# ConvFFN down: sixteen of its 22 blocks as seven products of 512 columns, with the sums of its weights made by DMA in DRAM

## The chip, the cores and the metric

One core of a Trainium2 chip runs the whole program. The metric is the device time of one execution in microseconds (us). Before the change the median of three runs is 840.73 us, from 840.38 to 840.88.

## The reference, cut to what matters

The reference is one decoder block on 512 tokens of 1024 channels: a conv branch and a gated recurrent branch are merged, projected and normalized (x1), and a ConvFFN follows. The change is in its last product and in the residual that is added to it:

```python
x = layer_norm(ALPHA * x + mix, ln1_g, ln1_b)
z = x @ w_ffn_in                        # 1024 -> 5632
u, gv = jnp.split(z, [D_FF], axis=-1)   # D_FF = 2816 = 22 blocks of 128
u = causal_dwconv(u, w_ffn_dw, b_ffn_dw)
y_ffn = (jax.nn.gelu(u) * gv) @ w_ffn_out   # 2816 -> 1024
x = layer_norm(ALPHA * x + y_ffn, ln2_g, ln2_b)
```

All of it is float32. The kernel multiplies in fp32r and splits each operand into a high part (a cast to fp32r) and a low part (the operand less its high part); a product is then three matmuls, high by high, high by low and low by high.

## The kernel before, in words

**Products.** `mm3` (L157) issues the three matmuls of a product (L159 to L161). `split` (L150) makes the two parts of an operand: ScalarE casts (L152), VectorE subtracts (L155).

**Weights.** All weights lie in one DRAM tensor of tiles of 128 x 1024 float32 (512 KB). `fetch(i)` (L113) loads tile i by SyncE's queue into a buffer `raw`, of which there are three (L119); ScalarE casts it to `hi` (L140) and VectorE subtracts to `lo` (L141). There are five buffers of `hi` and five of `lo`. For the tiles 8 to 67 the low part is made in another way (L127 to L129): ScalarE casts, ScalarE writes -hi into `lo`, and GpSimd issues a DMA that adds `raw` to `lo`; that tile's `raw` is free only when this DMA has landed. `weight(i)` (L144) fetches up to three tiles ahead.

**Order of the work.** The program is written in one order, and a planner puts the instructions of every engine and every DMA queue into a fixed order from that, by when its own model says that they are ready. Each queue then works strictly in order, and an instruction that waits holds up what is behind it.

**ConvFFN up** (L945 to L966). Blocks 0 to 2 are plain. For each of the blocks 3 to 21 the product is done with seven half-size products instead of eight (`seven`, L614; `seven_up`, L918). The sums of weights for that are made on VectorE (`weight_sums`, L583) from two tiles `d` and `e`, which SyncE's queue loads (L590): t13 is a difference of both (L594), t24 two more (L605, L606), and every one is split. `prepare(j + 1)` is written ahead of block j, so that a block's weights are made during the block before. Each block ends in `act` (L909), which writes the hidden block hT[j]. The last of the seven products of a block (`finish`, L656) is kept back in `pending` and issued inside the next block, since it adds to the bank X that VectorE has to read first (L654).

**ConvFFN down** (L969 to L1039). The 22 hidden blocks are split (`hidden`), and for the blocks k = 0 to 15 every weight tile is multiplied with four token blocks and two halves of 512 columns: 24 matmuls of 512 columns. Ahead of that stand two large loads: the 2 MB residual `x1a` from the DRAM copy `x1_d` (L978), and the four rows of gains and biases `lnp` (L970). The gain and bias of the first norm are put on the residual here (L1007, L1008). The `finish` of block 21 is issued after two of the four token blocks of k = 0 (L1017). The blocks 16 to 21 come last, token block by token block, each followed by its norm and its store.

Of the kernel before, what the change touches and what calls it, by code (L numbers as in the profile page):

```python
# [60 lines left out]
W_N = W_FO + 22  # L61


@with_exitstack
def hybrid_block(ctx: ExitStack, tc: tile.TileContext, wts: bass.AP, xT_d: bass.AP,
# [44 lines left out]

    resident = {}

    def fetch(i):  # L113
# [4 lines left out]
        for c in pieces:  # L118
            nc.sync.dma_start(raw[:, c], wts[i][:, c])  # L119
# [673 lines left out]

    x1_d = ctx.enter_context(tc.tile_pool(name="dram", bufs=1, space=bass.MemoryType.DRAM)).tile([T, D], F32, name="x1_d")
    x1 = [p1p.tile([P, 1024], F32, tag=f"oh{tb}", name=f"x1_{tb}") for tb in range(NT)]
# [26 lines left out]

    keep = {}

    def ln1_transposes(half, tb, n):
# [29 lines left out]
    for half in range(2):  # L855
# [11 lines left out]
        for tb in tbs:  # L867
# [3 lines left out]
            normalize(x1[tb], f"a{tb}")  # L871
            nc.sync.dma_start(x1_d[tb * P:tb * P + P, :], x1[tb])
# [5 lines left out]
    NK = 16  # L878
    hT = {}

    def hid():

        for tag, c0, n in [("ch", 0, 4), ("cl", 4, 4)] + [(f"sc{i}", 8 + 2 * i, 2) for i in range(4)]:
# [3 lines left out]
        for c in range(16, NFF):  # L887
            hT[c] = tmp.tile([P, T], F32, tag=("tot", "kt", "gg")[(c - 16) // 2], name=f"hT{c}")
# [40 lines left out]
    def prepare(j):  # L929
        i = W_FI + 2 * j  # L930
        if j in PLAINS:
# [5 lines left out]
            return [loaded.pop(i), loaded.pop(i + 1)]  # L937
        t = [p1p.tile([P, 1024], F32, tag=tag, name=f"T{tag}_{j}") for tag in ("oh2", "oh3")]
        b21 = [tmp.tile([P, T], F32R, tag=tag, name=f"b{tag}_{j}") for tag in ("kT", "t1")]
        return weight_sums(i, t, b21, ("oh0", "oh1"))  # L940

# [8 lines left out]
    for i in range(2):  # L950
        factor_sums(i, sh, sl)
    hid()
    for j in range(NF):
        act(j, *pss[2 * j:2 * j + 2])
    assert state[0] == W_FI + 2 * PLAIN, state
    for j in range(NF, NFF):
        if j == NF:
            w = prepare(j)
        wn = prepare(j + 1) if j + 1 < NFF else None
        if j in PLAINS:  # L960
# [7 lines left out]

    lnp = p1p.tile([P, 4, 1024], F32, tag="xl", name="lnp")  # L969
    po.dma_start(lnp, ln_d.unsqueeze(0).broadcast_to([P, 4, 1024]))  # L970
    bks = [4, 5, 0, 1, 2, 3, 6, 7]
    yps = {}

    res = p1p.tile([P, 4, 1024], F32R, tag="xh", name="fores")
    resident[W_FO + NK] = lambda: (res[:, 0], res[:, 1])
    resident[W_FO + NK + 1] = lambda: (res[:, 2], res[:, 3])
    x1a = p1p.tile([P, NT, 1024], F32, tag="ol", name="x1a")
    nc.sync.dma_start(x1a, x1_d.rearrange("(b p) c -> p b c", p=P))  # L978
    hres = [p1p.tile([P, 2, T], F32R, tag=f"sv{i}", name=f"hres{i}") for i in range(4)]
    hsp = {}  # L980

    def hidden(k):

        if k not in hsp:
            if NK <= k < NK + 4:
                hi, lo = hres[k - NK][:, 0], hres[k - NK][:, 1]
            else:
                if k % 2:
                    hl = tmp.tile([P, 2, T], F32R, tag="qq", name=f"hq{k}")
                    hi, lo = hl[:, 0], hl[:, 1]  # L990
                else:
                    hi, lo = [tmp.tile([P, T], F32R, tag=t, name=f"h{t}{k}") for t in ("kT", "t1")]
            split(hi, lo, hT[k])
            hsp[k] = (hi, lo)
        return hsp[k]

    def down(k, w, tb, ns=(0, 1)):
        hi, lo = hidden(k)
        ts = slice(tb * P, tb * P + P)
        for n in ns:  # L1000
            c = slice(n * 512, n * 512 + 512)
            mm3(yps[tb][n], (hi[:, ts], lo[:, ts]), (w[0][:, c], w[1][:, c]), k == 0, k == NFF - 1)

    for k in range(NK):
        if 2 <= k < 2 + NT:
            x_ = x1a[:, k - 2]
            ve.tensor_tensor(x_, x_, lnp[:, 0], ALU.mult)  # L1007
            ve.tensor_tensor(x_, x_, lnp[:, 1], ALU.add)  # L1008
        if k == 0:
            hidden(0)  # L1010
        w = weight(W_FO + k)
        for kk in range(k, min(k + 3, NK) if k else 1):
            hidden(kk)
        for tb in range(NT):
            if k == 0:
                if tb == 2:
                    pending.pop()()  # L1017
                yps[tb] = [bank(bks[2 * tb + n]) for n in range(2)]
            down(k, w, tb)
    ws = [weight(W_FO + k) for k in range(NK, NFF)]  # L1020
    for k in range(NK, NFF):
        hidden(k)
    for tb in range(NT):
        for n in range(2):
            for k in range(NK, NFF):
                down(k, ws[k - NK], tb, (n,))
        st = sml.tile([P, 2, 6], F32, tag="lst", name=f"lstb{tb}")
# [3 lines left out]
        for n, c in enumerate(halves):  # L1031
            ve.scalar_tensor_tensor(x1a[:, tb, c], x1a[:, tb, c], ALPHA, yps[tb][n], ALU.mult, ALU.add)
            ve.bn_stats(st[:, n], x1a[:, tb, c])
        ve.bn_aggr(mv, st.rearrange("p a b -> p (a b)"))
        rsqrt(rs, mv[:, 1:2], 1, 1.0, LN_EPS, f"b{tb}")
        for c in halves:
            ve.scalar_tensor_tensor(x1a[:, tb, c], x1a[:, tb, c], mv[:, 0:1], lnp[:, 2, c], ALU.subtract, ALU.mult)
            ve.scalar_tensor_tensor(x1a[:, tb, c], x1a[:, tb, c], rs, lnp[:, 3, c], ALU.mult, ALU.add)
            nc.sync.dma_start(out[tb * P:tb * P + P, c], x1a[:, tb, c])  # L1039


def pack(inp):
# [68 lines left out]
```

## Time and profile before

| | |
|---|---|
| median of three runs | 840.73 us |
| the profiled execution | 840.79 us, of which the span is 839.0 us |
| TensorE busy | 821.0 us of the span |
| VectorE, ScalarE, GpSimd busy | 617.0, 460.6 and 87.8 us |
| ConvFFN up, seven products | from about 517 us to 708.6 us, one block each 10.08 us |
| ConvFFN down | from 708.6 us to 830 us, then the norm of the last token block |

The span is the time from the first to the last instruction in the profile; the 1.8 us around it are in the run's time alone. PE stands for TensorE's matmuls, DVE for VectorE, ACT for ScalarE, POOL for GpSimd and SP for SyncE, whose name with a q is its DMA queue. Busy times overlap a little: a matmul is counted from its start until its result is out, though the next one starts before that, and so is a VectorE instruction. A rate is therefore read from starts that follow each other. In brackets a row gives how long the engine was idle before, and what ended it.

### The profile page before, as it was taken

The page shows a single profiled execution, that of the slowest core. Times are in us where ns is not written, and L with a number is a line of the kernel's source. Part 1 is how long each engine was busy: PE and PEld are TensorE (multiplying, and loading weights), DVE is VectorE, ACT ScalarE, POOL GpSimd, SP SyncE. Part 2 cuts the span into 40 slices and gives each one's busy share as a digit, 9 for nine tenths or more (in the row PEclk, how much of TensorE's full clock was granted, in tenths as well). Part 3 has the DMA queues.
Part 4 walks back from the last instruction along what each step waited for, and adds up shares of the span by engine and source line. Part 5 has one row for each costly group of instructions (what it writes and reads, how often), then busy time and mean ns, then how long its engine had stood idle before and what let it go on. Part 6 is the DMA issues. An engine that isn't in the chain of part 4 may idle for free.

```text
span 839.0 us, 14550 instructions
## 1 busy us (share of the span) xinstructions
PE 821.0 (98%) x5771; PEld 719.7 (86%) x5771; DVE 617.0 (74%) x1113; ACT 460.6 (55%) x820; POOL 87.8 (10%) x147
## 2 busy tenths in 40 slices
PE   8999999999999999999999999999999999999995
PEld 6888778777777778999978899999999999888884
DVE  5369999955587638788474689689998999844356
ACT  4455555667678865566641556566666666423200
POOL 0112431433332400000100000000000000000000
PEclk9999999999999999999999999999999999999998
DMA  8688666654543664233675332323333234634101
GB/s 287 177 180 206 167 148 155 166 135 128 130 126 98 170 171 138 76 104 110 162 242 187 115 113 76 95 84 104 118 106 101 101 102 161 271 121 130 46 26 75
DMA packets 32995, 113.40 MB, mean 135 GB/s; under 512 B 3616, under 2 KB 4512, under 8 KB 32800
## 3 DMA queue, kind: packets, MB, share of 16 engines
q1 hardware_dynamic: 24288, 82.85, 29.6%
q0 software_dynamic: 6480, 25.17, 14.9%
q10 hardware_dynamic: 2160, 4.47, 1.5%
q8 instruction: 45, 0.74, 0.4%
q14 instruction: 22, 0.18, 0.1%
HBM read 85.21 MB, written 4.19 MB: 107 GB/s over the span
## 4 chain that ended last, share of the span: by engine, by line
PE 78%; DVE 12%; ACT 4%; DMA 3%; issue 1%; DVEq 0%; ACTq 0%; POOLq 0%; SPq 0%
PE ps L159 25%; PE ps L160 24%; PE ps L161 24%; DVE cws L262 6%; DMA wr<-in_wts 2%; DMA xr<-in_xT 1%; PE ps L379 1%; ACT wh L127 1%; PE ps L528 1%; DVE tt L412 1%; PE ps L530 1%; PE ps L543 1%; DMA wl<-wr 1%; PE ps L517 1%; PE ps L492 0%
## 5 line engine op out<-in xcount | busy, mean ns | idle before, releaser
L159 PE MATMUL ps<-xh,wh 128*128 128x512 f32 x256 | 104.4, 409 | 0.5 <-ACT xh L152 0.4
L160 PE MATMUL ps<-xl,wh 128*128 128x512 f32 x256 | 100.9, 394 | 0.5 <-DVE xl L155 0.5
L161 PE MATMUL ps<-xh,wl 128*128 128x512 f32 x256 | 100.4, 392 | 0.0
L262 DVE SCALAR_TENSOR_TENSOR cws<-cws,par 128x512 f32<-128x512 f32 x120 | 84.8, 756 | 0.1
L140 ACT CAST wh<-wr 128x1024 fp32r<-128x1024 f32 x34 | 35.6, 1049 | 61.3 <-PE ps L161 34.3
L141 DVE TENSOR_TENSOR wl<-wr,wh 128x1024 fp32r<-128x1024 f32 (+1 forms) x38 | 43.2, 1139 | 34.7 <-ACT wh L140 34.4
L127 ACT CAST wh<-wr 128x1024 fp32r<-128x1024 f32 x44 | 46.4, 1057 | 39.1 <-PE ps L160 27.8
L159 PE MATMUL ps<-sh,shi_t 128*128 128x256 f32 x228 | 64.5, 283 | 0.0
L160 PE MATMUL ps<-sl,shi_t 128*128 128x256 f32 x228 | 64.5, 283 | 0.0
L161 PE MATMUL ps<-sh,slo_t 128*128 128x256 f32 x228 | 64.5, 283 | 0.0
L129 POOL DMA_DIRECT2D wl<-wr x44 | 38.6, 877 | 225.4 <-ACT wl L128 205.3
L159 PEld LDWEIGHTS ps<-xh,wh 128*128 128x128 f32 x256 | 48.2, 188 | 12.0 <-ACT xh L152 1.9
L161 PEld LDWEIGHTS ps<-xh,wl 128*128 128x128 f32 x256 | 48.1, 188 | 10.2
L160 PEld LDWEIGHTS ps<-xl,wh 128*128 128x128 f32 x256 | 48.2, 188 | 9.8 <-DVE xl L155 1.2
L155 DVE TENSOR_TENSOR slo_t<-Toh,shi_t 128x1024 fp32r<-128x1024 f32 x38 | 46.4, 1221 | 12.6 <-ACT shi_t L152 11.9
L152 ACT CAST shi_t<-Toh 128x1024 fp32r<-128x1024 f32 x38 | 39.9, 1050 | 16.7 <-PE ps L160 8.3
L128 ACT ACTIVATE wl<-wh 128x1024 fp32r<-128x1024 f32 x44 | 46.6, 1059 | 0.8
L159 PEld LDWEIGHTS ps<-sh,shi_t 128*128 128x128 f32 x228 | 43.8, 192 | 0.0
L160 PEld LDWEIGHTS ps<-sl,shi_t 128*128 128x128 f32 x228 | 43.8, 192 | 0.0
L161 PEld LDWEIGHTS ps<-sh,slo_t 128*128 128x128 f32 x228 | 43.8, 192 | 0.0
L568 ACT COPY pc<-ps 128x256 f32<-128x256 f32 x57 | 21.2, 372 | 37.0 <-PE ps L161 36.8
L155 DVE TENSOR_TENSOR slo_b<-wr,shi_b 128x1024 fp32r<-128x1024 f32 x27 | 32.9, 1218 | 2.4 <-ACT shi_b L152 2.4
(384 smaller groups left out, 2552.4 us busy)
## 6 DMA issues: line engine op xcount, KB each, us to landing
wr<-in_wts SPq DMA_DIRECT2D x141, 512.0 KB, 3.8
wl<-wr POOLq DMA_DIRECT2D x44, 512.0 KB, 4.9
xr<-in_xT ACTq DMA_DIRECT2D x8, 256.0 KB, 5.2
x<-in_x ACTq DMA_DIRECT2D x4, 512.0 KB, 9.9
x_d<-x SPq DMA_DIRECT2D x4, 512.0 KB, 4.1
x1a<-x_d SPq DMA_DIRECT2D x1, 2048.0 KB, 8.4
lnp<-in_ln POOLq DMA_DIRECT2D x1, 2048.0 KB, 10.6
out<-x1a SPq DMA_DIRECT2D x8, 256.0 KB, 2.0
```

What stands on the lines that cost most here:

```text
L127: ac.copy(hi, raw)
L128: ac.mul(lo, hi, -1.0)
L129: po.dma_start(lo, raw, accum_op=ALU.add)
L140: ac.copy(hi[:, c], raw[:, c])
L141: ve.tensor_tensor(lo[:, c], raw[:, c], hi[:, c], ALU.subtract)
L152: ac.copy(hi, src)
L155: (lo_eng or ve).tensor_tensor(lo, src, hi, ALU.subtract)
L159: pe.matmul(ps, a[0], b[0], start=start, stop=False, skip_group_check=more)
L160: pe.matmul(ps, a[0], b[1], start=False, stop=False, skip_group_check=more)
L161: pe.matmul(ps, a[1], b[0], start=False, stop=stop, skip_group_check=more)
L262: ve.scalar_tensor_tensor(cacc[j], cpad[j][:, i:i + T], w, cacc[j], ALU.mult, ALU.add)
L568: f(*args)
```

## The change: what it does, and its diff

- The blocks 0 to 15 of down are a product of 512 tokens by 2048 hidden channels by 1024 columns. It is cut in two in each of the three directions and done with seven products instead of eight. Each product has four weight tiles, and each tile gets 12 matmuls of 512 columns.
- Three of the seven weight operands are tiles of the input (b11, b21, b22). Four are sums of such tiles (t1 to t4): they are made in DRAM during up, by DMA copies on SyncE's queue and adding DMAs on GpSimd's. Four 64-byte DMAs ahead of the copies read hT[j-2], so that a copy can't go before that is written.
- So 34 tiles are fetched in down instead of 22. Of each four tiles the last (DMA_LOW) gets its low part by ScalarE, ScalarE and an adding DMA, like the tiles 8 to 67.
- The sums of hidden blocks (`operand`) are made on VectorE, and their parts by `split`. One of the two results of a token and column quarter is collected in the bank, the other is added to x1a on the way (`take_sum`).
- The gain and bias of the first norm go onto x1 before it is stored to x1_d (`residual`): for token blocks 0 and 1 among the steps that run beside up's start, for 2 and 3 (`late`) after `prepare(3)`. x1a now takes the buffer `xl`, which the `finish` of block 21 reads, and that `finish` is issued after three matmuls of down instead of twelve.

```diff
+FOP = ("b11", "b21", "t1", "t2", "b22", "t3", "t4")
+W_S = W_FO + 4 * len(FOP) + 6
+DMA_LOW = 3
...
+    def source(i):
+        if i < W_FO:
+            return wts[i]
+        n = i - W_FO
+        if n >= 4 * len(FOP):
+            return wts[W_FO + NK + n - 4 * len(FOP)]
+        t, m = FOP[n // 4], n % 4
+        return wts[W_FO + FO_OF[t] + m] if t in FO_OF else tsum[t][m]
...
-        if 8 <= i < W_OUT and i not in resident:
+        if (8 <= i < W_OUT or i >= W_FO and (i - W_FO) % 4 == DMA_LOW) and i not in resident:
...
+    def residual(tb):
+        ve.tensor_tensor(x1[tb], x1[tb], gb1[0], ALU.mult)
+        ve.tensor_tensor(x1[tb], x1[tb], gb1[1], ALU.add)
+        nc.sync.dma_start(x1_d[tb * P:tb * P + P, :], x1[tb])
...
+    def fo_sums(j):
+        fo = lambda t, m: wts[W_FO + FO_OF[t] + m]
+        m = j - NF - 1
+        if 0 <= m < 4:
+            for t, b in (("t1", "b12"), ("t3", "b12"), ("t2", "b22"), ("t4", "b21")):
+                nc.sync.dma_start(tsum[t][m][0:1, 0:16], hT[j - 2][0:1, 0:16])
+                nc.sync.dma_start(tsum[t][m], fo(b, m))
+        m, c = divmod(j - NF - 3, 3)
+        if 0 <= m < 4:
+            if c == 0:
+                po.dma_start(tsum["t1"][m], fo("b11", m), accum_op=ALU.add, max_dma_last_dim=4096)
+                po.dma_start(tsum["t3"][m], fo("b22", m), accum_op=ALU.add, max_dma_last_dim=4096)
+            elif c == 1:
+                po.dma_start(tsum["t2"][m], tsum["t1"][m], accum_op=ALU.add, max_dma_last_dim=4096)
+            else:
+                po.dma_start(tsum["t4"][m], tsum["t2"][m], accum_op=ALU.add, max_dma_last_dim=4096)
     for j in range(NF, NFF):
+        fo_sums(j)
         if j == NF:
             w = prepare(j)
+            for f in late:
+                f()
...
-    for k in range(NK):
...
-        for tb in range(NT):
...
-            down(k, w, tb)
+    ops = operand("b11")
+    for n, t in enumerate(FOP):
+        nxt = None
+        for m in range(4):
+            w = weight(W_FO + 4 * n + m)
+            if m == 1 and n + 1 < len(FOP):
+                nxt = operand(FOP[n + 1])
+            for c in range(2):
+                first, end = m == 0 and c == 0, m == 3 and c == 1
+                for i in range(2):
+                    if n == 0 and first:
+                        if i:
+                            pending.pop()()
...
+                    hi, lo = (o[:, c, i * P:i * P + P] for o in ops[m])
+                    cs = slice(c * 512, c * 512 + 512)
+                    mm3(C[i, into[t]], (hi, lo), (w[0][:, cs], w[1][:, cs]), new and first, end, not new)
+        for i in range(2):
+            take_sum(t, i)
+        ops = nxt
```

The banks of the four quarters are X, W and Z per token half: b11, t2, t3 and t4 go into X, b21 into W, t1 and b22 into Z; t2, b22, t3 and t4 add to what stands there. The six blocks behind the seven products and the norm are as before, but for the residual that has been added to three of the four quarters already, and for the rows of gain and bias, of which two (gb2) are loaded instead of four.

## Rows read from the trace of the kernel before

**Rows 1.** The page: the span, and the busy time of each engine.
```profile
span 839.0 us, 14550 instructions
PE 821.0 (98%) x5771; PEld 719.7 (86%) x5771; DVE 617.0 (74%) x1113; ACT 460.6 (55%) x820; POOL 87.8 (10%) x147
```
**Rows 2.** The chain of waits, 690 to 839 us: start us, us, what.
```profile
714.12 0.23 PE ps L161
...
737.24 0.23 PE ps L161
...
829.72 0.24 PE ps L161
829.99 0.70 DVE x1a L1032
...
835.08 0.66 DVEq L1107
```
**Rows 3.** Stretches of up and down: us, busy times (count), TensorE clock, DMA share, GB/s.
```profile
550.00:600.00 50.00, 50.00 (x419) 50.00 (x418) 45.21 (x59) 31.07 (x50) 0.00 (x0) 1.00 0.33 106
708.00:829.00 121.00, 121.00 (x544) 100.53 (x543) 69.43 (x104) 31.49 (x41) 0.56 (x1) 1.00 0.34 120
```
**Rows 4.** Groups by line and shape, 480 to 839 us: busy us, mean ns.
```profile
L141 DVE TENSOR_TENSOR wl<-wr,wh 128x1024 fp32r<-128x1024 f32 x20 | 24.4, 1222 | 21.8 <-ACT wh L140 21.7
L140 ACT CAST wh<-wr 128x1024 fp32r<-128x1024 f32 x20 | 20.9, 1048 | 28.8 <-PE ps L161 20.2 <-issue 4.1 <-DMA wr<-in_wts 3.8
```
**Rows 5.** The page's groups: ScalarE writes -hi into the low part.
```profile
L128 ACT ACTIVATE wl<-wh 128x1024 fp32r<-128x1024 f32 x44 | 46.6, 1059 | 0.8
```
**Rows 6.** VectorE in order of time, one block of up (555 to 582 us).
```profile
565.78 1.23 DVE L155 TENSOR_TENSOR slo_t<-Toh,shi_t 128x1024 fp32r<-128x1024 f32 x1 [0.80 <-ACT shi_t L152]
...
569.17 1.22 DVE L594 TENSOR_TENSOR Toh<-wr,wr 128x1024 f32<-128x1024 f32 x1
...
572.12 1.22 DVE L155 TENSOR_TENSOR slo_b<-wr,shi_b 128x1024 fp32r<-128x1024 f32 x1
573.25 0.68 DVE L606 TENSOR_TENSOR Toh<-wr,Toh 128x512 f32<-128x512 f32 x1
573.85 1.22 DVE L155 TENSOR_TENSOR slo_t<-Toh,shi_t 128x1024 fp32r<-128x1024 f32 x1
```
**Rows 7.** ScalarE in order of time, the same block.
```profile
567.09 0.62 ACT L152 CAST bkT<-wr 128x512 fp32r<-128x512 f32 x1 [0.21 <-DMA wr<-in_wts]
```
**Rows 8.** DMA queues, 150 to 300 us: packets, MB, share of 16 engines.
```profile
q0 software_dynamic: 2736, 9.96, 34.2%
q1 hardware_dynamic: 2880, 10.22, 20.3%
```
**Rows 9.** Line 119, 150 to 300 us: issue to landing of the weight loads.
```profile
DMA to landing us min/median/max: 3.3/3.4/5.8
```
**Rows 10.** Line 129, 150 to 300 us: GpSimd's issues (ns), and their landing.
```profile
L129 POOL DMA_DIRECT2D wl<-wr x20: 855/879/1122, 151.7 to 299.2; - x20
...
DMA to landing us min/median/max: 4.4/4.8/7.4
```
**Rows 11.** ScalarE, 437 to 450 us: casts of weight tiles that come each 2.7 us.
```profile
442.03 1.05 ACT L140 CAST wo_ol<-wr 128x1024 fp32r<-128x1024 f32 x1 [2.18 <-DMA wr<-in_wts]
444.70 1.05 ACT L140 CAST wh<-wr 128x1024 fp32r<-128x1024 f32 x1 [1.62 <-DMA wr<-in_wts]
448.13 1.05 ACT L140 CAST wh<-wr 128x1024 fp32r<-128x1024 f32 x1 [2.38 <-DMA wr<-in_wts]
```
**Rows 12.** The start of down as a stretch, columns as in group 3.
```profile
716.00:720.00 4.00, 4.00 (x19) 3.33 (x18) 3.31 (x5) 2.24 (x4) 0.00 (x0) 1.00 1.05 440
```
**Rows 13.** ScalarE at the start of down.
```profile
723.39 1.05 ACT L140 CAST wh<-wr 128x1024 fp32r<-128x1024 f32 x1 [3.76 <-DMA wr<-in_wts]
```
**Rows 14.** TensorE where up ends and down begins.
```profile
708.50 0.28 PE L161 MATMUL ps<-sh,slo_t 128*128 128x256 f32 x1
708.62 0.40 PE L159 MATMUL ps<-wh,hkT 128*128 128x512 f32 x1
...
711.37 0.28 PE L159 MATMUL ps<-x1h,shi_t 128*128 128x256 f32 x1
```
**Rows 15.** VectorE at the same place.
```profile
709.31 0.41 DVE L568 TENSOR_TENSOR ug<-ps,pc 128x256 f32<-128x256 f32 x1
```
**Rows 16.** VectorE early in up.
```profile
526.01 0.69 DVE L652 TENSOR_TENSOR ug<-ps,pc 128x512 f32<-128x512 f32 x1 [1.60 <-PE ps L161]
```

More of the change, by code (lines that the diff above doesn't have):

```diff
@@ L823, in hybrid_block @@
     keep = {}
+    late = []
     def ln1_transposes(half, tb, n):
@@ L875, in hybrid_block, with hid @@
                 steps.append(lambda half=half, tb=tb, n=n: ln1_transposes(half, tb, n))
-    NK = 16
+            (late if half else steps).append(lambda tb=tb: residual(tb))
     hT = {}
-    def hid():
-        for tag, c0, n in [("ch", 0, 4), ("cl", 4, 4)] + [(f"sc{i}", 8 + 2 * i, 2) for i in range(4)]:
+    hT2 = []
+    def hid(part):
+        for tag, c0, n in ([("ch", 0, 4), ("cl", 4, 4)], [(f"sc{i}", 8 + 2 * i, 2) for i in range(4)])[part]:
             t_ = p1p.tile([P, n, T], F32, tag=tag, name=f"hT{tag}")
@@ L886, in hid @@
                 hT[c0 + c] = t_[:, c]
-        for c in range(16, NFF):
+            for c in range(0, n, 2):
+                hT2.append(t_[:, c:c + 2])
+        for c in range(16, NFF) if part else ():
             hT[c] = tmp.tile([P, T], F32, tag=("tot", "kt", "gg")[(c - 16) // 2], name=f"hT{c}")
@@ L951, in hybrid_block @@
         factor_sums(i, sh, sl)
-    hid()
+    hid(0)
     for j in range(NF):
@@ L979, in hybrid_block @@
[L979 to L986, printed above, removed]
-            else:
[L988 to L995, printed above, removed]
@@ L997, in down @@
-    def down(k, w, tb, ns=(0, 1)):
-        hi, lo = hidden(k)
+    x1a = p1p.tile([P, NT, 1024], F32, tag="xl", name="x1a")
+    nc.sync.dma_start(x1a, x1_d.rearrange("(b p) c -> p b c", p=P))
+    gb2 = [tmp.tile([P, 1024], F32, tag="qq", name=f"gb2_{i}") for i in range(2)]
+    for i in range(2):
+        po.dma_start(gb2[i], ln_d[2 + i:3 + i].broadcast_to([P, 1024]))
+    halfT = {}
+    for q in range(4):
+        halfT["a11", q], halfT["a21", q] = hT2[q][:, :, 0:256], hT2[q][:, :, 256:512]
+        halfT["a12", q], halfT["a22", q] = hT2[4 + q][:, :, 0:256], hT2[4 + q][:, :, 256:512]
@@ new lines, in operand @@
+    def operand(t):
+        out = []
+        for q in range(4):
+            g = lambda a: halfT[a, q]
+            if t == "t1":
+                src = s12[q]
+                ve.tensor_tensor(src, g("a21"), g("a22"), ALU.subtract)
+            elif t == "t2":
+                src = s12[q]
+                ve.tensor_tensor(src, src, g("a11"), ALU.subtract)
+            elif t == "b22":
+                src = g("a12")
+                ve.tensor_tensor(src, src, s12[q], ALU.add)
+            elif t == "t3":
+                src = g("a21")
+                ve.tensor_tensor(src, g("a11"), src, ALU.subtract)
+            else:
+                src = g({"b11": "a11", "b21": "a12", "t4": "a22"}[t])
+            o = homes[t][q](t)
+            split(o[:, 0], o[:, 1], src)
+            out.append((o[:, 0], o[:, 1]))
+        return out
@@ new lines, in hybrid_block, with rows, take_sum @@
+    C = {(i, n): None for i in range(2) for n in "XWZV"}
+    bks = dict(zip([(i, n) for n in "XWZV" for i in range(2)], [4, 5, 0, 1, 2, 3, 6, 7]))
+    into = {"b11": "X", "b21": "W", "t1": "Z", "t2": "X", "b22": "Z", "t3": "X", "t4": "X"}
+    def rows(i, half, n):
+        return x1a[:, 2 * half + i, n * 512:n * 512 + 512]
+    def take_sum(t, i):
+        if t in ("b11", "t1", "t2"):
+            x_ = rows(i, *{"b11": (0, 0), "t1": (1, 1), "t2": (0, 1)}[t])
+            ve.scalar_tensor_tensor(x_, x_, ALPHA, C[i, into[t]], ALU.mult, ALU.subtract if t == "t2" else ALU.add)
+        elif t == "t3":
+            x_ = rows(i, 1, 1)
+            ve.tensor_tensor(x_, x_, C[i, "X"], ALU.subtract)
@@ new lines, in hybrid_block @@
+    hres = p1p.tile([P, 4, 2, T], F32R, tag="ol", name="hres")
+    hid_ = []
+    for k in range(NK, NFF):
+        o = hres[:, k - NK] if k < NK + 4 else p1p.tile([P, 2, T], F32R, tag=("at", "oh0")[k - NK - 4], name=f"hres{k}")
+        split(o[:, 0], o[:, 1], hT[k])
+        hid_.append((o[:, 0], o[:, 1]))
+    resident[W_S - 1] = lambda: tuple(p1p.tile([P, 1024], F32R, tag=f"sv{1 + i}", name=f"fol{i}") for i in range(2))
+    ws = [weight(W_S - 6 + k) for k in range(6)]
+    for i in range(2):
+        C[i, "V"] = bank(bks[i, "V"])
@@ L999, in down @@
+    yps = [[C[0, "W"], C[0, "Z"]], [C[1, "W"], C[1, "Z"]], [C[0, "X"], C[0, "V"]], [C[1, "X"], C[1, "V"]]]
+    for tb in range(NT):
         ts = slice(tb * P, tb * P + P)
-        for n in ns:
+        for n in range(2):
             c = slice(n * 512, n * 512 + 512)
-            mm3(yps[tb][n], (hi[:, ts], lo[:, ts]), (w[0][:, c], w[1][:, c]), k == 0, k == NFF - 1)
-    for k in range(NK):
[L1005 to L1013, printed above, removed]
-        for tb in range(NT):
[L1015 to L1018, printed above, removed]
-            down(k, w, tb)
@@ L1020, in hybrid_block @@
[L1020 to L1026, printed above, removed]
+            fresh = tb >= 2 and n == 1
+            for k in range(6):
+                mm3(yps[tb][n], (hid_[k][0][:, ts], hid_[k][1][:, ts]), (ws[k][0][:, c], ws[k][1][:, c]), fresh and k == 0,
+                    k == 5, not fresh)
         st = sml.tile([P, 2, 6], F32, tag="lst", name=f"lstb{tb}")
```

58 lines of the change are left out of this document (40 added, 18 removed).

## The prediction, made before the changed kernel was run

> **What bounds the kernel now.** I read the page's busy times first: TensorE works 821.0 of 839.0 us [rows 1]. The chain of waits then shows that from 708.6 us on the end is set by matmuls alone: one row ends each 0.23 us until 829.96, and behind them stands VectorE's norm of the last token block, about 9 us [rows 2]. The stretches say the same of up and down: TensorE has no gap and its granted clock is 1.00, the upper of its two levels, 2.4 GHz [rows 3]. So a matmul taken out is time taken out, as long as TensorE doesn't wait instead; the other engines and the DMA queues cost nothing until they are late. What the reader should look for is how near they are: VectorE is busy 45.2 of 50 us in up, 69.4 of 121 in down.
>
> The sum is made against the profiled execution, 840.79 us (span 839.0 and 1.8 around it); the median of the runs is 840.73, so the two count as one. About 0.2%, 1.7 us, is what a measurement can tell from no change.
>
> **What is removed.** Sixteen blocks had 16 x 4 x 2 x 3 = 384 matmuls; seven products of four tiles have 28 x 2 x 2 x 3 = 336. From 714.12 to 737.24 us lie 34 groups of three [rows 2], 0.680 us each, 0.2267 us a matmul. The 48 that go are worth **10.9 us**. A weight tile now lasts 12 matmuls, 2.72 us, instead of 5.44, and a product 10.88 us. Fewer matmuls can't give more than this, so 829.9 is the floor; the norm at the end keeps its instructions.
>
> **What is added, term by term.**
>
> *The kept-back product of block 21.* It needs the bank that VectorE reads until 709.31 + 0.41 = 709.72 [rows 15]. Up's last matmul starts at 708.50, down's first at 708.62, and the kept-back product came at 711.37, long after [rows 14]. With three matmuls ahead instead of twelve it would come at 708.62 + 0.68 = 709.30: a wait of **0.4 us**. Ends: 0 if other matmuls are planned ahead of it, 1.6 if VectorE is inside another instruction of 1.22.
>
> *Bank X between t3 and t4.* t4 adds to the bank that VectorE has to read after t3. The first token half is complete 0.68 us before the second, and a read takes 0.7; VectorE starts 0.03 us after the last matmul where it is free [rows 2]. So nearly nothing, or 1.3 if it is busy: **0.3 us**. The other reads of a bank have a whole product, 10.88 us.
>
> *VectorE and ScalarE in the seven products.* Instructions start 1.13 us (1024 columns) and 0.60 us (512) after each other [rows 6]. A product wants three low parts of weights (3.4), four of the next operand (2.4), for four of the seven four sums (2.4), and two reads of a bank (1.4): at most 9.6 of 10.88 us. A block of up has 10.08 us with 0.80 idle [rows 6] and TensorE doesn't wait there, so 9.6 alone costs **nothing**. ScalarE has 4 x 1.05 + 1.06 + 4 x 0.62 = 7.7 us [rows 4, 5, 7].
>
> *The weight tiles of down.* From 150 to 300 us the weight queue took 20.3% of 150 us for 10.22 MB and the adding queue 34.2% for 9.96 MB [rows 8]: 1.56 us of all engines per 512 KB load, 2.70 per adding DMA. A product wants 4 x 1.56 + 2.70 = 8.9 of 10.88 us. The narrow place is the three raw buffers. A plain tile holds one for 3.4 us of load [rows 9], 1.05 of cast, 1.22 of subtraction [rows 4] and 0.6 of handing over (an estimate, from the gaps of 0.21 and 0.80 in [rows 6, 7]), 6.3 us; every fourth for 3.4 + 1.05 + 1.06 + 4.8 [rows 10] + 0.6 = 10.9. Three plain and one slow tile make 29.8, over three buffers 9.9 us a product: it fits, with one us to spare, at median landings. Halfway to the longest ones (5.8 and 7.4) the tiles hold 7.5, 7.5, 7.5 and 13.4, in all 11.9 a product, 1.0 too much. The nearest rows with such a rate are the casts at 442, 444.7 and 448.1 us, each waiting for its load: one tile in 3.05 us [rows 11]. That pace for 28 tiles would cost 28 x 0.33 = 9.2 us, the upper end; the lower is 0. Down starts with up to five tiles split and three landing, but the 2 MB of x1a and 1 MB of gb2 (six times 1.56, 9.4 us) come then: before, with 4 MB, the engines were full [rows 12] and a cast waited 3.76 us [rows 13], which a tile of 5.44 us hid and one of 2.72 won't. I take **2.5 us**, nearer to the fitting sum, since the casts at 442 us had other large loads beside them.
>
> In the rows GpSimd's issue of an adding DMA lasts 0.86 to 1.12 us, beside a busy VectorE [rows 10]; the spread of 0.27 us is all that VectorE can have cost there, and I charge nothing more. The Trainium skill, page "SBUF — State Buffer", section "Who interferes with whom", says that a VectorE instruction with two SBUF inputs shuts out a GpSimd instruction that reads SBUF until it ends. By the row the sum stays, by that rule it is the rival on late issues below, if issuing counts as reading.
>
> *The six last blocks.* Tile 31 has its low part by DMA too, and its buffer is that of tile 26, free at the start of 27: 2.72 us until the last stage and 2.27 until its use there, 5.0 us, for 1.05 + 1.06 + 4.8 + 0.6 = 7.5. That is 2.5 late (5.1 at the longest landing), or 0 where another column half is planned ahead: **1 us**.
>
> *VectorE in up.* The gain and bias, eight instructions of 1.13, move from down's start into up: half to where it is idle, 4.5 us ahead of block 4. The first gap behind is 1.60 us [rows 16]. Ends 0 and 2.9. Together with the next item: **1 us**.
>
> *The DMAs in up.* Sixteen copies at 1.56 are 25 us and sixteen additions at 2.70 (the price with both sides in SBUF; in DRAM no row shows it) 43, beside a DMA share of 0.33 [rows 3]: two thirds of up's 190 us are free, so there is room on average. Locally four copies stand in SyncE's queue near a load that is used at once: ScalarE waits 0.21 us for it [rows 7]. VectorE wants it 2.1 us later (569.17), and its parts are ready at 573.3 [rows 6] for a block that starts at 577.6 (708.6 less 13 blocks of 10.08): 4.3 us more. So a single delay of 6.4 us is hidden, and four copies are 6.2.
>
> **Sum:** 840.8 - 10.9 + 0.4 + 0.3 + 2.5 + 1 + 1 = **835.1 us**.
>
> **Rivals.**
>
> *All hidden.* The terms at their lower ends: 829.9 to 832. For it: the rate of the raw buffers fits at medians and VectorE has managed 92% in up. Chance 0.18.
>
> *The raw buffers set the pace.* Every tile comes at 3.05 us: 829.9 + 9.2 + 2.7 for the other terms, 841.8. For it: rows 11. Against it: the lead at the start. It decides once a landing is 1 us above its median throughout. 0.15, most of it no change.
>
> *Slower: the copies put up's weight loads late.* Place: blocks 4 to 7. If the four copies are planned ahead of the load in SyncE's queue, VectorE falls behind by 6.2 - 2.1 = 4.1 us in each of the four blocks and regains 0.8 in each: 13.2, of which 4.3 are free. TensorE waits 8.9 us: 834.1 + 8.9 = **843.0**. It decides as soon as this happens in two blocks on end, or where a copy or an addition in DRAM costs twice its price here. For it: the load is used 0.2 us after it lands, and longer landings are seen where queues share the engines (5.8 against 3.4). Against it: only if the planned order is that one. The Trainium skill, page "DMA: Bandwidth & Descriptors", section "Queues, rings and completion order", says that an engine takes turns between its queues packet by packet; by that rule the additions too would stretch each load beside them, and for more blocks than four. 0.15.
>
> *The sums aren't there.* Four chains of three additions of 4.8 us, 58 us from about 537, end at 595; t1 is fetched at about 720. Only additions three times as slow reach that; the first load of t1 would then wait, some 845. 0.03.
>
> *Late issues.* If each of the eight adding DMAs of down waits for one VectorE instruction of 1.13, the slow tiles hold their buffers that much longer, and at worst all of it reaches TensorE: 835.1 + 9.0 = 844.1. The spread of 0.27 us [rows 10] speaks against it. 0.03. The rule of the page "SBUF — State Buffer" in the Trainium skill, above, is what would do it.
>
> **How the numbers follow.** My forecast has 0.46 (832 to 839), the rivals 0.18, 0.15, 0.15, 0.03 and 0.03. Faster by over 0.2% (under 839.0): 0.46 + 0.18 and 0.02 of the raw buffers, 0.66. Within: 0.10 of the raw buffers and 0.02 of the copies, 0.12. Slower: 0.03 + 0.13 + 0.03 + 0.03, 0.22. The range 830 to 846 takes in the floor, both stalls in full and half of a dearer copy.
>
> **What would show it.** Right: TensorE's matmuls 48 fewer and 10.9 us less of chain; in up a gap of no more than 1 us; in down gaps of a few tenths at product boundaries, with casts that wait for loads now and then. The raw buffers: ScalarE's casts in down waiting for loads in every product. The copies: L594 waiting for its load and TensorE idle between 527 and 570. I am wrong if TensorE is idle for over 8 us in up and down together, or if its clock falls in a gap, which the rows here, at 1.00, don't show.

## The result and the profile after

The changed kernel takes **867.8 us** (median of four runs, 865.1 to 870.0) against 840.6 for the kernel before: ratio **1.032, 95% interval 1.029 to 1.035**. It is slower by 27 us, where 5.7 us of gain were forecast. A kernel's ratio goes by its fast runs alone, those within 1.5% of its fastest; only e3 below has others.

The profiled execution took 868.95 us. Its page: span, busy times, the two lines on the chain that ended last, and the landing of the sums' adding DMAs.

```profile
span 867.1 us, 14668 instructions
PE 826.1 (95%) x5723; PEld 720.9 (83%) x5723; DVE 642.5 (74%) x1153; ACT 486.8 (56%) x852; POOL 107.9 (12%) x172
...
PE 55%; DMA 18%; DVE 16%; ACT 6%; issue 4%; SPq 0%; DVEq 0%; ACTq 0%; POOLq 0%
...
t<-in_wts POOLq DMA_DIRECT2D x8, 512.0 KB, 12.6
t<-t POOLq DMA_DIRECT2D x8, 512.0 KB, 7.6
```

TensorE has its 48 matmuls fewer (5723 against 5771 in [rows 1]) and is busy 5 us longer, so that many of them last longer; the granted clock below shows why. The chain, which was matmuls alone in [rows 2], goes through DMAs. Next the stretches of up and down, with the columns of [rows 3].

```profile
530.00:620.00 90.00, 78.22 (x583) 76.02 (x582) 60.58 (x79) 41.78 (x68) 13.14 (x16) 0.91 0.93 250
620.00:730.70 110.70, 110.70 (x924) 110.68 (x923) 104.94 (x137) 71.57 (x115) 0.00 (x0) 1.00 0.34 114
730.70:858.30 127.60, 117.27 (x494) 95.00 (x492) 83.84 (x132) 56.46 (x72) 8.07 (x10) 0.95 0.64 192
```

While the sums are made (530 to 620 us) the DMA engines are busy 0.93 instead of 0.33 [rows 3], TensorE gets 583 matmuls done and the mean clock is 0.91; from 620 us on up runs as before. Down is disturbed throughout.

How early up begins differs by a few tenths up to 4 us from run to run (its first matmul of 256 columns starts at 482.25 us in the trace of before, at 483.82 here). So I compare lengths: *up* from that matmul to down's first one of 512 columns, *down* from there to the end of the last matmul. Before: 226.4 and 121.3 us. After: **246.9 and 127.4**. The 28.1 us of span are 20.5 in up, 6.0 in down (where 10.9 were to go away, so 16.9 of loss) and 1.6 ahead of up.

**Up.** TensorE at its largest gap, in order of time (in brackets how long it was idle, and what ended that):

```profile
558.67 0.28 PE L179 MATMUL ps<-sh,slo_b 128*128 128x256 f32 x1
563.89 0.58 PE L177 MATMUL ps<-sh,shi_t 128*128 128x256 f32 x1 [4.94 <-ACT pc L586]
564.27 0.41 PE L178 MATMUL ps<-sl,shi_t 128*128 128x256 f32 x1
564.48 0.41 PE L179 MATMUL ps<-sh,slo_t 128*128 128x256 f32 x1
```

It doesn't wait for its weights but for L586, a copy by which ScalarE empties a bank. ScalarE at the same place:

```profile
562.94 0.62 ACT L170 CAST bkT<-wr 128x512 fp32r<-128x512 f32 x1 [8.29 <-DMA wr<-in_wts]
563.47 0.37 ACT L586 COPY pc<-ps 128x256 f32<-128x256 f32 x1
```

The copy takes 0.37 us, and it stood behind a cast that waited 8.29 us for a weight load. TensorE used that cast's result only at 568.94 us; the copy it wanted at once. The waits from 530 to 620 us say that this is the pattern (total us, times, longest):

```profile
ACT bkT L170 <- DMA wr<-in_wts: 23.3, 5, 8.3
DVE Toh L612 <- DMA wr<-in_wts: 19.1, 5, 7.4
```

And the DMA queues from 540 to 600 us (packets, MB, share of 16 engines) say why loads were late: the additions on q0 took as much of the engines as everything on SyncE's q1.

```profile
q1 hardware_dynamic: 1526, 10.36, 47.3%
q0 software_dynamic: 1380, 5.00, 46.3%
```

A gap is counted here from start to start, less the usual distance of two matmuls. TensorE's gaps of over 0.3 us make 13.0 us in up. Three of the eight, 8.1 us, end with that copy. In the other five, 4.9 us in two blocks, TensorE waits for its weights themselves: their loads came so late that the parts made from them weren't ready in time. ScalarE's cast had waited 5.53 us for its load in the first of the two blocks (579.35 us) and 2.54 in the second (594.69).

```profile
580.02 0.39 PE L177 MATMUL ps<-x1h,bkT 128*128 128x256 f32 x1 [0.85 <-ACT bkT L170]
...
584.56 0.58 PE L179 MATMUL ps<-sh,slo_t 128*128 128x256 f32 x1 [1.25 <-DVE slo_t L173]
...
596.91 0.38 PE L179 MATMUL ps<-x1h,bt 128*128 128x256 f32 x1 [1.04 <-DVE bt L173]
```

The other 7.5 us are mostly matmuls at half clock: in the first rows above they follow each other by 0.21 instead of 0.12 us. In stretches of 2 us, the granted clock is the number behind the five busy times:

```profile
560.00:562.00 2.00, 0.00 (x0) 0.00 (x0) 0.00 (x0) 0.00 (x0) 0.00 (x0) 0.95 1.05 272
562.00:564.00 2.00, 0.11 (x1) 0.11 (x1) 1.05 (x1) 0.89 (x2) 0.61 (x1) 0.50 1.06 270
564.00:566.00 2.00, 2.00 (x10) 2.00 (x11) 2.00 (x4) 1.76 (x3) 0.21 (x1) 0.50 1.07 195
566.00:568.00 2.00, 2.00 (x11) 2.00 (x11) 2.00 (x4) 1.22 (x2) 0.00 (x0) 0.50 1.05 211
```

**Down.** Its gaps, TensorE in order of time:

```profile
740.46 0.39 PE L177 MATMUL ps<-wh,sosv_b 128*128 128x512 f32 x1
743.20 0.50 PE L178 MATMUL ps<-wl,sosv_b 128*128 128x512 f32 x1 [2.35 <-DMA wl<-wr]
...
757.17 0.79 PE L178 MATMUL ps<-wl,sooh_b 128*128 128x512 f32 x1 [2.79 <-DMA wl<-wr]
...
808.09 0.47 PE L177 MATMUL ps<-wh,soxh_t 128*128 128x512 f32 x1 [1.78 <-DVE x1a L1089]
...
825.60 0.80 PE L178 MATMUL ps<-wl,hres 128*128 128x512 f32 x1 [3.22 <-DMA wl<-wr]
```

Three are the adding DMA of a slow tile (the last is tile 31, in the six last blocks), one is bank X between t3 and t4. With what follows them directly they make 11.5 us; at half clock a matmul of 512 columns takes 0.43 instead of 0.2267, for 13 of them behind the second gap and 12 behind the last, 25 x 0.195 = 4.9 us. Together 16.4 of the 16.9. The clock again:

```profile
742.00:744.00 2.00, 0.80 (x3) 0.67 (x4) 0.84 (x2) 0.89 (x2) 0.00 (x0) 1.00 1.01 399
...
758.00:760.00 2.00, 2.00 (x6) 1.52 (x6) 1.53 (x3) 1.53 (x2) 0.00 (x0) 0.50 0.90 285
...
826.00:828.00 2.00, 2.00 (x6) 1.52 (x6) 0.00 (x0) 0.00 (x0) 0.00 (x0) 0.50 0.00 0
```

The chain shows what keeps the slow tiles late: the first one's adding DMA lands after 10.34 us (at 4.7 in the median), beside `x1a` and `gb2`. Then one slow tile follows the other, since the load of the next one goes into the buffer that the last one frees: it is issued as that adding DMA lands (803.47). The adding DMAs are issued 10.7 to 12.3 us after each other from the second on (775.58 to 787.85, 798.81 to 809.49), where a product without gaps takes 10.88.

```profile
732.82 10.34 DMA wl<-wr
...
775.58 4.69 DMA wl<-wr
780.28 5.03 DMA wr<-in_wts
...
785.38 2.45 issue
787.85 4.63 DMA wl<-wr
...
798.81 4.64 DMA wl<-wr
...
803.47 3.49 DMA wr<-t
...
807.02 2.45 issue
...
809.49 4.68 DMA wl<-wr
```

### The profile page after: what moved, and what is told of

It reads as the page before. It is cut to its first block, busy times and chain, and to the rows that moved or that the text cites. A ratio compares the mean times of both kernels' runs of the same rounds, so it can differ in the third digit from the quotient of the medians.

```text
span 867.1 us, 14668 instructions
## 1 busy us (share of the span) xinstructions
PE 826.1 (95%) x5723; PEld 720.9 (83%) x5723; DVE 642.5 (74%) x1153; ACT 486.8 (56%) x852; POOL 107.9 (12%) x172
## 4 chain that ended last, share of the span: by engine, by line
PE 55%; DMA 18%; DVE 16%; ACT 6%; issue 4%; SPq 0%; DVEq 0%; ACTq 0%; POOLq 0%
PE ps L177 17%; PE ps L178 17%; PE ps L179 17%; DMA wr<-in_wts 10%; DVE cws L280 6%; DMA wl<-wr 5%; DMA wr<-t 2%; DMA xr<-in_xT 1%; PE ps L397 1%; DVE wl L159 1%; DVE slo_t L173 1%; ACT wh L145 1%; PE ps L546 1%; DVE tt L430 1%; PE ps L548 1%
## 5 line engine op out<-in xcount | busy, mean ns | idle before, releaser
L147 POOL DMA_DIRECT2D wl<-wr x52 | 45.6, 878 | 417.1 <-ACT wl L146 271.1
L145 ACT CAST wh<-wr 128x1024 fp32r<-128x1024 f32 x52 | 54.8, 1056 | 45.5 <-PE ps L178 28.7
L159 DVE TENSOR_TENSOR wl<-wr,wh 128x1024 fp32r<-128x1024 f32 (+1 forms) x43 | 49.3, 1149 | 38.5 <-ACT wh L158 38.2
L177 PE MATMUL ps<-sh,shi_t 128*128 128x256 f32 x228 | 67.1, 294 | 7.7 <-ACT pc L586 7.6
L158 ACT CAST wh<-wr 128x1024 fp32r<-128x1024 f32 x39 | 40.8, 1047 | 59.0 <-DMA wr<-in_wts 30.7
L179 PE MATMUL ps<-sh,slo_t 128*128 128x256 f32 x228 | 66.5, 292 | 1.3 <-DVE slo_t L173 1.2
L178 PE MATMUL ps<-sl,shi_t 128*128 128x256 f32 x228 | 66.3, 291 | 0.0
L177 PEld LDWEIGHTS ps<-xh,wh 128*128 128x128 f32 x256 | 48.4, 189 | 12.3 <-ACT xh L170 2.2
L146 ACT ACTIVATE wl<-wh 128x1024 fp32r<-128x1024 f32 x52 | 55.1, 1060 | 1.0
L178 PEld LDWEIGHTS ps<-sl,shi_t 128*128 128x128 f32 x228 | 45.7, 200 | 0.0
L586 ACT COPY pc<-ps 128x256 f32<-128x256 f32 x57 | 20.8, 372 | 30.7 <-PE ps L179 29.6
L612 DVE TENSOR_TENSOR Toh<-wr,wr 128x1024 f32<-128x1024 f32 x19 | 23.2, 1220 | 19.1 <-DMA wr<-in_wts 19.1
## 6 DMA issues: line engine op xcount, KB each, us to landing
t<-in_wts POOLq DMA_DIRECT2D x8, 512.0 KB, 12.6
```

The lines of the kernel that those rows point to most:

```text
L177: pe.matmul(ps, a[0], b[0], start=start, stop=False, skip_group_check=more)
L178: pe.matmul(ps, a[0], b[1], start=False, stop=False, skip_group_check=more)
L179: pe.matmul(ps, a[1], b[0], start=False, stop=stop, skip_group_check=more)
L612: ve.tensor_tensor(t13.rearrange("p (a c) -> p a c", a=2), e[:, H[0]].unsqueeze(1).broadcast_to([P, 2, 512]), d.rearrange("p (a c) -> p a ...
```

## The experiments

All against the kernel before, run on the same chip at the same time; up and down are the lengths defined above, from the profiled execution.

| kernel | us, median (all) | ratio, 95% | up | down |
|---|---|---|---|---|
| before | 840.6 to 841.3 | 1 | 226.4 | 121.3 |
| the change | 867.8 (865.1 to 870.0) | 1.032, 1.029 to 1.035 | 246.9 | 127.4 |
| e1 no sums | 847.8 (847.4 to 848.2) | 1.008, 1.006 to 1.010 | 226.5 | 128.7 |
| e2 copies only | 848.6 (846.5 to 850.2) | 1.009, 1.007 to 1.011 | 226.8 | 128.8 |
| e3 copies on GpSimd's queue | 874.4 (862.1 to 877.9) | 1.032, 1.024 to 1.039 (of the runs 862.1 and 873.1) | 251.8 | 127.1 |
| e4 no slow tiles | 855.4 (853.6 to 862.3) | 1.019, 1.014 to 1.023 | 252.7 | 116.4 |
| e6 no sums, no slow tiles | 834.8 (833.0 to 838.2) | 0.992, 0.989 to 0.995 | 226.5 | 114.7 |
| e7 no slow tiles, other order | 854.8 (851.4 to 855.2) | 1.015, 1.012 to 1.018 | 249.6 | 111.7 |
| e5 sums spread | 848.4 (847.0 to 851.0) | 1.008, 1.006 to 1.011 | 228.6 | 125.8 |
| e11 spread, no slow tiles | 839.1 (834.6 to 841.7) | 0.997, 0.995 to 0.999 | 230.4 | 116.4 |
| e8 spread, no slow tiles, order | 836.8 (836.1 to 838.2) | 0.994, 0.992 to 0.997 | 228.9 | 113.5 |
| e9 the change, fourth raw buffer | 856.7 (855.9 to 859.1) | 1.019, 1.017 to 1.021 | 239.6 | 124.0 |
| e12 is e8 with the buffer | **830.2** (830.1 to 830.6) | **0.987, 0.986 to 0.989** | 226.4 | 110.7 |
| e10 is e12 and a later product | 830.7 (830.6 to 831.0) | 0.988, 0.986 to 0.989 | 226.4 | 110.7 |

### What in the sums puts up late

My theory after the result (A): the additions fill the DMA engines and make up's weight loads late. Rival (B): copies and 64-byte DMAs hold up the loads in SyncE's queue. **e1** takes all of it away:

```diff
-        fo_sums(j)
-        return wts[W_FO + FO_OF[t] + m] if t in FO_OF else tsum[t][m]
+        return wts[W_FO + FO_OF[t] + m] if t in FO_OF else wts[W_FO + FO_OF["b12"] + m]
```

> Leaves out the DMA copies and additions during up; t1 to t4 are read from an input tile instead, so the values of the seven products are not the reference's, while every load, cast, subtraction and matmul of down stays. Theory (up lost 22.1 us because of these DMAs): up ends where it ended before, near 709 us, and the time is about 867.8 - 22 = 846 us. Rival (the gain and bias moved into up made VectorE late): up still ends after 720 us and the time stays above 858.

The stretch from 500 to 620 us has no idle TensorE left:

```profile
500.00:620.00 120.00, 120.00 (x1003) 120.00 (x1002) 109.89 (x147) 76.04 (x120) 0.00 (x0) 1.00 0.31 102
```

Up is as long as before (226.5). So the gain and bias that moved into up cost nothing, and all 20.5 us are the sums'. Down stays long, with five gaps at slow tiles (2.17, 2.41, 0.93, 0.91, 0.97), 1.99 at bank X and 4.35 at tile 31. **e2** keeps the copies alone:

```diff
-        if 0 <= m < 4:
+        if 0 > 1:
             if c == 0:
                 po.dma_start(tsum["t1"][m], ...
```

> Leaves out the sixteen additions (the sums are not made); copies and their 64-byte DMAs stay in SyncE's queue. Theory A (the DMA engines are full: copies 25 us and additions 46 us of them, the loads land late): with a third of that work left, up loses under 7 us, time 846 to 853. Theory B (order of SyncE's queue: up's loads stand behind the copies, which wait for the landing of the 64-byte DMAs): up still loses 15 us or more, time 860 to 868.

Up is 226.8 with no gap: the copies, in the very places that were suspected, cost nothing. **e3** keeps everything and frees SyncE's queue of them:

```diff
-                nc.sync.dma_start(tsum[t][m][0:1, 0:16], hT[j - 2][0:1, 0:16])
-                nc.sync.dma_start(tsum[t][m], fo(b, m))
+                po.dma_start(tsum[t][m][0:1, 0:16], hT[j - 2][0:1, 0:16])
+                po.dma_start(tsum[t][m], fo(b, m))
```

> All copies, 64-byte DMAs and additions stay, but the copies and 64-byte DMAs are issued from GpSimd's queue, so nothing waits in SyncE's queue ahead of up's loads. Theory A (full engines): the same bytes in the same blocks, up still loses 12 us or more, time above 857. Theory B (order of SyncE's queue): up loses under 5 us, time 846 to 851.

Up is 25.4 us longer than before, with gaps of 6.12, 2.23, 5.88 and 2.47, all behind L586. The loads of L608 are alone in their queue now and land even later (min, median, max; 3.4, 4.0 and 5.3 in the trace of before):

```profile
DMA to landing us min/median/max: 5.4/9.8/14.0
```

B falls, A stands: what matters is how much else the engines have to move at that time, whichever queue it stands in. The additions without the copies weren't run, so their shares of the 20.5 us aren't parted; the copies alone cost nothing.

### What the slow tiles cost down

**e4** makes every low part of down's weights on VectorE; **e6** does that without the sums (e1's edit too).

```diff
-DMA_LOW = 3
+DMA_LOW = -1
```

> Only the way of the low part changes: all 34 tiles of down get theirs from VectorE, none from an adding DMA. Theory (down's three gaps of 2.5, 2.9 and 3.4 us that wait for a low part made by DMA, and the half clock after two of them): down gets 12 to 15 us shorter, time 853 to 856. Rival (VectorE then is the limit: 4 x 1.13 + 2.4 + 2.4 + 1.4 = 10.7 of 10.88 us a product): down stays within 3 us, time 865 to 871.

> Leaves out the copies and additions (t1 to t4 read from an input tile, so the values of the seven products are not the reference's) and gives all tiles of down their low part on VectorE. Theory (the losses of up and of the slow tiles are two things and add up): 847.8 - 12.4 = 835 us, 833 to 838. Rival (the slow tiles cost only because up's backlog of DMA runs into down): no better than without sums alone, 845 to 849.

Down falls from 127.4 to 116.4 us (11.0, a little under the theory's 12 to 15), and from 128.7 (e1) to 114.7. The only gap over 0.8 us left in down is bank X's, 3.44 and 2.19 us. 847.8 - 834.8 = 13.0 us is the price of the eight slow tiles; what tile 31 alone costs wasn't tried. Seven products without a low part by DMA fit on VectorE, for which the prediction's 9.6 of 10.88 us, with three low parts a product, had left room: in e12 VectorE is busy 66.7 of the 76.2 us of the seven products (the first row), and TensorE doesn't wait in all of down (the second).

```profile
708.70:784.90 76.20, 76.20 (x344) 63.15 (x343) 66.71 (x85) 47.25 (x62) 1.14 (x2) 1.00 0.69 235
708.70:819.50 110.80, 110.78 (x494) 91.22 (x492) 91.45 (x138) 49.46 (x64) 1.14 (x2) 1.00 0.53 181
```

**e7** also moves t4 away from t3, so that another product lies between the two that share bank X:

```diff
-FOP = ("b11", "b21", "t1", "t2", "b22", "t3", "t4")
+FOP = ("b11", "t1", "t2", "b21", "t3", "b22", "t4")
-    homes = {..., "b21": four("sv1", "sv2", "sv3", "oh2"),
+    homes = {..., "b21": four("at", "oh0", "oh1", "sv0"),
```

> All low parts on VectorE as in the run without slow tiles (855.4 us), and the order of the products b11, t1, t2, b21, t3, b22, t4, so that no two that add to bank X follow each other; t3 and b21 get operand buffers that allow it. Theory (the last gap of down, 3.4 us, is t4 waiting for VectorE's read of X after t3, and the clock is at half behind it): 4 to 6 us less than 855.4, 849 to 852. Rival (VectorE is late there by as much whatever the order): 854 to 857.

The gap is gone and down is 4.7 us shorter than in e4 (111.7), yet the medians differ by 0.5 only, and the two intervals overlap: with the sums as they are, up varies by more than that from run to run. The time, 854.8, lies in the rival's range; by time this stayed open until e11.

### Spreading the sums

**e5** keeps all 16 copies and 16 additions, but one of each per block in blocks 4 to 20, instead of four copies in each of the blocks 4 to 7 and the additions close behind:

```diff
-        m = j - NF - 1
-        if 0 <= m < 4:
...
+        s = j - NF - 1
+        if 0 <= s < 16:
+            m, c = divmod(s, 4)
+            t, b = (("t1", "b12"), ("t2", "b22"), ("t4", "b21"), ("t3", "b12"))[c]
+            nc.sync.dma_start(tsum[t][m][0:1, 0:16], hT[j - 2][0:1, 0:16])
+            nc.sync.dma_start(tsum[t][m], fo(b, m))
+        s -= 1
+        if 0 <= s < 16:
+            m, c = divmod(s, 4)
+            t, b = (("t1", fo("b11", m)), ("t2", tsum["t1"][m]), ("t4", tsum["t2"][m]), ("t3", fo("b22", m)))[c]
+            po.dma_start(tsum[t][m], b, accum_op=ALU.add, max_dma_last_dim=4096)
```

> Same sixteen copies and sixteen additions, but one copy and one addition per block of up, over blocks 4 to 20, instead of four copies a block in blocks 4 to 7 and additions as soon as those land. Theory (the additions are too dense: from 540 to 600 us they and the copies want 64 us of DMA engine time in 60): a block then wants 3.1 + 1.5 + 2.9 = 7.5 of 10.08 us, up loses under 4 us, time 847 to 851. Rival (every addition makes the load beside it late, however far apart they are): up loses 10 us or more, time above 857.

The same bytes cost up 2.2 us instead of 20.5. **e8** is e5 with e7's edits, **e11** is e5 without slow tiles in the old order:

> All three together: additions spread over blocks 4 to 20, no slow tiles, products in the other order. It computes all of the reference. If the three losses (up's additions 20 us, slow tiles 12.4, bank X 5) are separate, 867.8 - 37 = 831 us, 830 to 835, and faster than the kernel before by 0.7 to 1.3%. If the spread additions still make loads late, 838 or more.

> The sums spread evenly over up, and no low part of down's weights by DMA; the products stay in the order of the change (t3 directly before t4). Against the kernel of the same kind with the other order, 836.8 us, this shows what the bank X between t3 and t4 costs when up is quiet. Theory: t4's first matmul waits 2 to 3.4 us for VectorE, which takes t3's result out of X, and the granted clock is at half for some us behind it: 839 to 842 us. Rival: the wait costs nothing that is not given back by tiles that are then ready earlier: 836 to 838 us.

e8 is the first kernel that beats the one before and computes all of the reference; its 836.8 us lies between the two theories, and up is still 2.6 us longer than before. Against e8, e11's down is 2.9 us longer (116.4 and 113.5), with a gap of 2.38 at bank X, and its median 2.3 us higher; its runs spread over 7 us, so the size is rough. ScalarE and VectorE beside that gap, in e11:

```profile
781.01 1.05 ACT L158 CAST wh<-wr 128x1024 fp32r<-128x1024 f32 x1 [1.88 <-DMA wr<-t]
782.09 1.23 DVE L159 TENSOR_TENSOR wl<-wr,wh 128x1024 fp32r<-128x1024 f32 x1 [1.71 <-ACT wh L158]
783.23 1.28 DVE L1085 TENSOR_TENSOR x1a<-x1a,ps 128x512 f32<-128x512 f32 x2
```

VectorE wasn't busy, it stood 1.71 us at a low part whose load was late, and the reading of the bank was queued behind that. It is up's pattern again, on the other engine.

### One raw buffer more

e8 still lost 2.6 us in up, in gaps of 0.46, 0.36 and 0.82 behind L586 and shorter ones. There a load can be issued only when one of three raw buffers comes free. **e9** gives the second load of every odd block of up a free tile for its own, in the kernel of the change; **e12** does it in e8:

```diff
-            raw.append(wp.tile([P, 1024], F32, tag="raw", name=f"wr{i + c}", bufs=3))
+            if c and extra and i % 4:
+                raw.append(p1p.tile([P, 1024], F32, tag="at", name=f"wr{i + c}"))
+            else:
+                raw.append(wp.tile([P, 1024], F32, tag="raw", name=f"wr{i + c}", bufs=3))
```

> The changed kernel, where the second weight load of every odd block of up gets a raw buffer of its own, so that up has four instead of three (the sums, the slow tiles and the order of the products stay). Theory: the additions hurt because up's loads are issued only when one of three raw buffers comes free, a few us before ScalarE wants them, so that each late landing stands in front of the bank copies in ScalarE's queue; a load that is issued about half a block earlier is late less often. Up then ends less than 12 us later than before instead of 22.1, and the time is 852 to 860 us. Rival: between 540 and 600 us the DMA engines are simply asked for more than they can do, and an earlier issue only lengthens the queue: up still ends 18 us or more later, time 863 or above.

> The kernel with the spread sums, no low part of down's weights by DMA and the products in the other order (836.8 us), plus the fourth raw buffer in up alone; the kept-back product of block 21 stays after three matmuls of down. It parts the two edits that together brought 836.8 down to 830.7. Theory: the buffer does nearly all of it, because ScalarE's cast waited 30.1 us in 14 places for its weight load without it and 3.5 us in 3 with it, and behind those casts stood the copies that TensorE waits for: 831 to 832.5 us, down's first matmul within 1 us of 708.6, and a gap of about 0.6 at the kept-back product. Rival: the later place of the kept-back product is what mattered, by another order of down's instructions: 834 to 836.5 us.

e9 takes 7.3 us from up, leaving 13.3 of the 20.5, against the 12 that the theory allowed: the buffer helps, but where the engines are full it can't do enough. Where they have room, it does all. Who waited for L608's loads in up, from 530 to 720 us, in e8:

```profile
  ACT bkT L170: 30.1, 14
  DVE Toh L612: 9.0, 7
```

and for the same loads (now L611) from 530 to 700 us in e12, with their landing:

```profile
  ACT bkT L170: 6.9, 4
...
DMA to landing us min/median/max: 4.6/6.5/9.8
```

The loads land no sooner (5.2 in the median in e8); they are asked for earlier: in e12 the cast at 620.98 us came 7.6 us after its load was issued and didn't wait for it, in e8 the one at 622.86 came 5.6 us after and had waited 1.90. Up is at its length of before although the engines are twice as busy, and down is 110.7:

```profile
530.00:620.00 90.00, 90.00 (x752) 90.00 (x752) 80.80 (x106) 55.78 (x90) 5.72 (x7) 1.00 0.69 199
```

**e10** also issues the kept-back product of block 21 after six matmuls of down instead of three:

```diff
+                    if n == 0 and m == 0 and c and not i:
+                        pending.pop()()
                     if n == 0 and first:
-                        if i:
-                            pending.pop()()
```

> The whole of the reference, with everything that helped so far: sums spread evenly over up (one copy and one addition a block), no low part of down's weights by DMA, the products in the order b11, t1, t2, b21, t3, b22, t4, the fourth raw buffer in up, and the kept-back product of block 21 after six matmuls of down instead of three. Theory: the order alone with these stood at 836.8; the remaining gaps of TensorE were 0.82 in up and 0.64 at the kept-back product, and these two go: 834 to 836 us, ratio 0.991 to 0.995. Rival: what is left above 831 does not come from gaps of that size but from the run-to-run spread of up with the DMA engines partly shared, and the time stays at 836.5 to 838.

It came out better than either theory said. But e12, which ran last, has the old place of that product and the same time and lengths: the buffer did it, a little better than its theory said, and in e12 that product comes after five matmuls without a gap. Of e12's gain on e8 2.5 us lie in up, where the buffer acts, and 2.8 in down, where e8 had gaps at the kept-back product (0.65) and at weights of the last blocks (1.8) and e12 has none. Why the buffer ends these too is not shown; it may be another order of the plan.

## Why the prediction was wrong, point by point

- **What is removed: right.** 10.9 us were to go from down; in e12, where nothing waits, down is 121.3 - 110.7 = 10.6 shorter. The floor of 829.9 was nearly reached, at 830.2, by another kernel.
- **VectorE and ScalarE in the products, VectorE in up, late issues: right.** No run shows a loss from the gain and bias in up (e1) or from VectorE's work in the products (e12); where TensorE waited about 1.0 us for a low part from VectorE in down (e5, e8, e9), the cast ahead of it had waited for a load. GpSimd's issues of the eight slow tiles took 0.853 to 0.912 us beside VectorE. The rule of the Trainium skill, page "SBUF — State Buffer", section "Who interferes with whom", which would bear on them only if issuing counts as reading, left no mark on them.
- **The DMAs in up: the step that failed most, at most 1 us (together with the gain and bias) against 20.5 us.** The prices were good: an addition in DRAM took 2.9 to 3.2 us of all engines (2.95 in e12, 530 to 620 us: 26.2% of 90 us for 8 of them), where I took 2.70. "There is room on average" was true too: e12 has the same work with a share of 0.69 and no loss. What failed stands in two sentences. One: I spread the work over up's 190 us, but nearly all of it ran between 530 and 620, and from 540 to 600 us q0 and q1 together took 94% of the engines. Two: "a single delay of 6.4 us is hidden" counted from the load to the block that uses the weights. It wasn't one delay: ScalarE's cast waited five times between 530 and 620 us, up to 8.3, and in two blocks the weights themselves came late (4.9 of the 13.0 us of gaps). And I never asked what is queued behind the waiting cast on ScalarE. It is the copy that empties TensorE's bank, and for that the slack is next to nothing (8.1 of the 13.0 us). The remaining 7.5 us are mostly the clock.
- The rival of late weight loads had the right loads, but the wrong cause, the copies (e2), less than half of the price, and a place that ended too early: it looked for idle TensorE between 527 and 570 us, and 7.3 of the 13.0 us of gaps came later, up to 613. The sentence beside it was nearer: the Trainium skill, page "DMA: Bandwidth & Descriptors", section "Queues, rings and completion order", has an engine take turns between its queues packet by packet; by that rule additions stretch every load beside them. The trace fits that, with 1526 and 1380 packets and 47.3% and 46.3% of the engines' time for the two queues from 540 to 600 us; it doesn't show the turns themselves. I had weighed it at 0.15 together with the rest.
- **The raw buffers: 2.5 taken, 9.2 as the upper end; 13.0 measured with tile 31's part (e1 less e6).** My 10.9 us for a slow tile was nearly right (10.7 to 12.3 in the trace after the second). Sharing that evenly over three buffers was the error: one slow tile follows the other in a line, each taking about a product's 10.88 us or more, and such a line can't make up the late start that I had seen coming (10.34 us beside `x1a` and `gb2`). Tile 31's wait of 2.3 to 4.2 us in the six kernels with slow tiles lay within 0 to 5.1, above the 1 us that I took.
- **Bank X: 0.3 taken, 1.3 at most; gaps of 0.6 to 3.4 us in the kernels with t4 behind t3, 1.7 or more in all but e9 (0.6) and e5, where a cast ended it (1.15)**; and 2.9 us of down's length between e11 and e8. I let VectorE be free or busy; it was waiting: the low part ahead of its reading of the bank stood for its cast 3.96 us in the change, 4.19 in e1, 1.74 in e4, 1.78 in e6 and 1.71 in e11.
- **The kept-back product: right** to a few tenths (no gap in the change and in e12, about 0.6 in e5, e8 and e11).
- **The clock: no term at all.** It cost about 7 us in up and 4.9 in down. That a gap might bring it down was named as a way to be wrong, but priced at nothing; that sign came, and so did the other, TensorE idle for over 8 us (24.5 us of gaps in up and down together). The Trainium skill has the effect, on page "TensorE: Matmul & The Clock Gate", section "HAM oscillation — how this bites in real kernels": waits for DMAs put the clock to half, and the matmuls behind them pay for it. The rows here agree, at 0.50.

## What to carry to other kernels

Count the slack of a late load at every engine that waits for it, not at the final use: on an engine that works in order, the next instruction in its queue, here a bank copy of 0.37 us, inherits the whole wait. Put DMA work that nobody is in a hurry for evenly over the stretch that has room, and give the loads beside it one more buffer; 16 copies and 16 additions cost 20.5 us bunched, 2.2 to 4.0 spread (e5, e8, e11), and nothing spread and with a fourth raw buffer. A line of dependent transfers that takes its whole period (here 10.7 to 12.3 of 10.88 us) has no way to regain a late start.

## What was not expected

- Gaps of 2.95 and 3.37 us in down were followed by 13 and 12 matmuls at a granted clock of 0.50, those of 2.51 and 1.94 us by none, so that a gap of 3 us cost about 6; in up the clock was at 0.50 even behind a gap of 2.40 (613 us), some blocks after longer ones. The gap's length alone doesn't tell: in e1's down 7 matmuls at half clock followed a gap of 2.17 us (0.50 from 722 to 724 us) and none one of 2.41.
- An adding DMA with both sides in DRAM took little more of the engines (2.9 to 3.2 us for 512 KB) than one with both in SBUF (2.70, [rows 8]), but landed after 5.6 to 7.0 us in the median in the kernels with spread sums, and after 7.6 and 12.6 in the change, where the engines were full.
